# Padded small products, a first loop over three groups, a shorter rsqrt chain and new ranks in a hybrid decoder layer

## The chip, the cores and the metric

The kernel runs on one core of one Trainium2 chip. Its engines are TensorE (PE, matrix products; PEld is the loading of its weights), VectorE (DVE), ScalarE (ACT), GpSimd (POOL) and SyncE (SP, which issues most transfers). Each works through its own instructions in a fixed order and waits on counters that other engines and transfers raise. The metric is device time in microseconds of one execution, as the median over runs.

## The reference

One inference step of one layer, for a prompt of 512 tokens and for eight running sequences of one new token each (called sample), all in fp32. The columns of one input projection belong to two mixers: gated linear attention (GLA: qa, ka, va, the low-rank forget gate za and the output gate ga) and dilated attention over past keys (qb, kb, vb, gb).

```python
h = jnp.einsum('btd,de->bte', x, w_in)
qa, ka, va, za, ga, qb, kb, vb, gb = jnp.split(h, split_points, axis=-1)
log_a = jax.nn.log_sigmoid((jnp.einsum('btr,rk->btk', za, w_alpha2) + b_alpha)) / GATE_TEMP
o_a, s_new = gla_chunked(qa, ka, va, log_a, s0, chunk)        # S_t = diag(a_t) S_{t-1} + k_t^T v_t, o_t = q_t S_t
o_a = o_a * lax.rsqrt(jnp.mean(jnp.square(o_a), axis=-1, keepdims=True) + RMS_EPS) * gla_norm_g
o_b = prompt_dilated(qb, kb, vb, rel_bias)                    # sample: dilated_attention over the cache and the new row
mix = jnp.concatenate([o_a * jax.nn.silu(ga), o_b * jax.nn.silu(gb)], axis=-1)
x_new = layer_norm(DEEPNORM_ALPHA * x + jnp.einsum('bte,ed->btd', mix, w_out), ln_g, ln_b)
```

Dilated attention has 8 heads of 64; each evaluates three patterns (window, dilation) (128,1), (512,4), (2048,16) with a relative position bias from 32 buckets, and the three outputs are merged by their softmax denominators. Outputs are the new x of prompt and sample, both GLA states, and the new key and value rows.

## The kernel before

**Precision.** An fp32 product of the large projections is made of three matmuls on fp32r operands: each operand is split into a high part (a cast) and a low part (the difference), and hi x hi, lo x hi and hi x lo are added up in PSUM (`three`, line 618). The cast runs on ACT (`hi_...`, `xx<-x_raw`), the subtraction on DVE (`lo_...`, `xx<-x_raw,xx`). Small products, called here small, run directly on fp32 operands.

**Stages.** `dense` (line 691) is PE's main stream: eight matmuls on a zeroed tile for warming up (`warm_ps`), then the first loop, then za, qa, qb, kb, vb, gb, va, ga and the output projection (`ps_yf`, `ps_y`), behind which stand residual and layer norm (`norm`, line 1593). x is held transposed: 1024 rows in eight tiles of 128, with 520 columns, 512 of the prompt and 8 of sample; it is worked in two halves of 264 and 256 columns.

**The first loop** has both groups of 128 columns of ka: for each of the eight tiles of the inner dimension, two halves times two groups times three matmuls, 96 in all, on four PSUM banks. Its loads come in the order of `FIRST` (line 542), issued by SP; the first tiles of x and of the weights come in small pieces. The splits follow in the same order (`first_splits`, line 573). ACT also issues four small loads of `wz` (`clear`, line 532); its table of functions is loaded once (line 1615).

**Sample's small products.** Beside the stream stand small fp32 products: `ps_qk` (in `sample_past`), `ps_sl` and `ps_pn` (logits and new-row weights in `sample_softmax`), `ps_ov` (in `sample_gla`, whose result goes through `o_r` on DVE and a norm to a transpose, `ps_ort`), and `ps_ms` and `ps_vs` (mean and variance in `residual_sample`). Their operands have 32 or 64 rows or columns.

**Order.** All instructions but a few are issued by one line, 366, of a planner (`Plan`, line 198): the code is written as some forty tasks (Python generators) with a rank each, `add(task(), rank)`, lower first. The planner keeps a model of the engines' times and issues, at build time, the instruction that can start first; ties go by rank. `dense` has rank 100, so it fills PE wherever no other task's product is ready. So ranks alone decide where in an engine's order small work stands. `SLOTS` is the number of buffers of each size (for example `sv`, the 512 KB tiles of sample's past keys and values; `w`, split weights; `r`, raw weights; `g`, larger results), `BANKS` the PSUM banks by use. Every transfer raises one of eight counters, taken in turn (`DMAHW0` to `DMAHW7`); a transfer that is the next to use a counter waits on the queue of its issuing engine until the one before on this counter has landed.

**Sample's attention** runs past keys and values through POOL: `past` times the broadcast query (`qbc`) gives logits that DVE reduces (`lt`), then `vv` times the broadcast probabilities (`pb`) gives values that DVE reduces (`o_pv`).

**rsqrt** (line 395) is Exp(-0.5 Ln(x)) with a Newton step; in `norm` it gets `between`, the task that centres y on DVE while ACT works.

Of the kernel before, what the change touches and what calls it, by code (L numbers as in the profile page):

```python
# [59 lines left out]
N_WARM = 8  # L60

SLOTS = dict(
    g=23,
    w=6, r=3,
    sv=5,
    pt=4,
    t2=3, st=3,
    pr=6,
    t1=5, ob=4,
# [7 lines left out]
SWITCH = 105  # L77
PIECE = 256
# [116 lines left out]
class Plan:  # L195
# [3 lines left out]
    def __init__(self, nc):  # L199
        self.engines = {n: Engine(n, e) for n, e in (("PE", nc.tensor), ("DVE", nc.vector), ("ACT", nc.scalar),  # L200
                                                     ("POOL", nc.gpsimd), ("SP", nc.sync))}
        self.dma = 0.0
        self.tasks, self.marks = [], defaultdict(int)
        self.slots, self.slot_of, self.uses, self.shares = {}, {}, defaultdict(dict), {}
        self.seq = self.issued = 0
# [48 lines left out]
    def ready(self, op):  # L254
        t = 0.0
        for write, aps in ((False, op.reads), (True, op.writes)):
            for x in aps:
                _, p0, p1, f0, f1 = self.region(x, write)
                for ((w, q0, q1, g0, g1), e), end in self.uses[x.tensor.name].items():
# [3 lines left out]
                    if (w if same else w or write) and p0 < q1 and q0 < p1 and f0 < g1 and g0 < f1:  # L263
# [65 lines left out]
    def begin(self, op, ready):  # L329
# [7 lines left out]
        start = max(eng.free, ready)  # L337
# [6 lines left out]
    def issue(self, op, start):  # L344
# [12 lines left out]
        if unit == "SP":  # L357
# [4 lines left out]
            end += self.dma  # L362
        for write, aps in ((False, op.reads), (True, op.writes)):
# [7 lines left out]
def trunk(ctx: ExitStack, tc: tile.TileContext, xT, xp, xs, state, ck, cv, w_in, wab, gnorm,  # L371
# [23 lines left out]
    def rsqrt(o, x, scale, eps, between=None):  # L395

        t = yield Need("m", "newton", [P, size(x)])
        t = t[:x.ap[0][1]]
        yield V.tensor_scalar(x, x, scale, eps, op0=ALU.mult, op1=ALU.add)
        yield S.activation(o, x, AF.Ln)  # L400
        yield S.activation(o, o, AF.Exp, scale=-0.5)
        if between:

            add(between, 5)
            yield S.activation(t, o, AF.Square)
            yield S.mul(t, t, x)
            yield S.activation(t, t, AF.Copy, scale=-0.5, bias=1.5)
            yield S.mul(o, o, t)
        else:
            yield V.tensor_tensor(t, o, o, op=ALU.mult)  # L410
# [23 lines left out]
    rb = cst("rb", [66, NB, HB], F32R)  # L434
# [8 lines left out]
    lt = cst("lt", [P, 2, 64])  # L443
# [68 lines left out]
    order = [g for k, g in groups.items() if k not in ("ka0", "ka1")] + wo  # L512
# [17 lines left out]
    one16 = cst("one16", [P, 1])  # L530

    def clear():
# [5 lines left out]
        for j in range(4):  # L538
# [3 lines left out]
    FIRST = (("x", 0, TS[0]), ("w", 0, 1), ("x", 0, TS[1]), ("w", 1, 2), ("x", 1), ("w", 2, 4), ("x", 2), ("x", 3),  # L542
             ("w", 4, 6), ("x", 4), ("x", 5), ("w", 6, 8), ("x", 6), ("x", 7))
    ka_raw = []

    def first_loads():
        za = w_in[:, OFF["za"]:OFF["za"] + 16].rearrange("(k p) n -> p k n", p=P)
        for n, a, *b in FIRST:
# [5 lines left out]
            else:  # L554
                if a % 4 == 0:
                    ka_raw.append((yield Need("r", f"raw_ka{a}", [P, 4, GW])))
                rows = w_in[a * P:b[0] * P, OFF["ka"]:OFF["ka"] + GW]
                yield D.dma_start(ka_raw[a // 4][:, a % 4:a % 4 + b[0] - a, :], rows.rearrange("(k p) n -> p k n", p=P))
# [4 lines left out]
        add(weight_loads(), 3)  # L563
# [9 lines left out]
    def first_splits():  # L573
        for j, (n, a, *b) in enumerate(FIRST):
# [10 lines left out]
            else:  # L585
                if a % 4 == 0:
                    hl = []
                    for x in ("hi", "lo"):
                        hl.append((yield Need("w", f"{x}_ka{a}", [P, 4, GW], F32R)))
                    ka_hl.append(hl)  # L590
                    for i in range(2):
                        g = groups[f"ka{i}"]
                        for l, y in zip((g.hi, g.lo), hl):
                            l += [y[:, k, i * P:i * P + P] for k in range(4)]
                r = slice(a % 4, a % 4 + b[0] - a)
                yield from split(ka_raw[a // 4][:, r, :], *(y[:, r, :] for y in ka_hl[a // 4]))
                for _ in range(a, b[0]):
                    mark("kas")
                if b[0] % 4 == 0:
                    free(ka_raw[a // 4])  # L600
        add(weight_splits(), 19.3)

    def fills():
        yield V.memset(rb.bitcast(F32)[64:66], 1.0)
# [86 lines left out]
    def dense():  # L691
# [6 lines left out]
        for i in range(2):  # L698
            for u in range(2):
                pk[i, u] = yield bank("ds"[i], f"ps_ka{i}{u}")  # L700
        for k in range(KT):
            for u in range(2):
                yield At("kas", k + 1)
                yield At("xs", k + 1 + (u if k == 0 else 1))
                for i in range(2):
                    yield from three(pk[i, u][:, :TW[u]], k, halves(k, u, groups[f"ka{i}"]))
# [9 lines left out]
        add(gate_decay(pz), 10)  # L716
        yield from make("ka", Need("g", "ka", [P, 2, NP]), 3)
        yield from make("qa", Need("g", "qa", [P, 2, NP]), 2)
        for i in range(2):
            for u in range(2):  # L720
                add(into("ka", ka_s, i, 1.0)(pk[i, u], u), 2)
        for i in range(2):
            yield from feature(groups[f"qa{i}"], into("qa", qa_s, i, 0.125))
# [18 lines left out]
        for t in range(TT):  # L742
            add(residual(t), 8)
        add(residual_sample(), 8)
# [8 lines left out]
    def gate_decay(pz):  # L753
# [21 lines left out]
        for j in (0, 1, 4, 2, 3):  # L775
            z, o, to = parts_[j]
            yield S.activation(o, z, AF.Abs)
# [36 lines left out]
    def gla_levels():  # L814
# [6 lines left out]
        for li, h in enumerate(LEVELS):  # L821
# [21 lines left out]
            if li % 2:  # L843
                add(gla_level(made), 22)
# [171 lines left out]
    def parts(n, own, m, scale):  # L1016

        def evac(ps, u):
# [5 lines left out]
            yield V.scalar_tensor_tensor(l, ps[:, :256], scale, h.bitcast(F32), op0=ALU.mult, op1=ALU.subtract)  # L1024
            if u == 0:
                yield S.mul(own[:, m, :], ps[:, 256:TW[0]], scale)
            mark(f"{n}b{m}{u}")
            mark(f"{n}b")
            if n == "k":
                add(keys_out(ps, m, u), 2)  # L1030
# [25 lines left out]
    def sample_v(x, n, out):  # L1056
        yield At(n, 4)
        rows = yield Need("t1", n + "_rows", [32, P])
        yield from sample_rows(x, rows)
        yield D.dma_start(out, rows)  # L1060
# [148 lines left out]
    def sample_queries():  # L1209
# [3 lines left out]
        for bi in range(NB):  # L1213
# [4 lines left out]
            add(sample_logit(bi, past, qbc), 50)  # L1218
# [10 lines left out]
    def sample_softmax():  # L1229
        yield At("kb", 8)  # L1230
        yield At("lt", 5)
        sel = yield Need("t1", "sel", [64, C_AV - C_E2])
        yield D.dma_start(sel, c_f[:64, C_E2:C_AV])
        e2, pnm, m32 = sel[:, :P], sel[:, C_PN - C_E2:C_PN - C_E2 + 32], sel[:32, C_LN - C_E2:]
# [522 lines left out]
```

## Time and profile before

| | |
|---|---|
| time, median of 3 runs | 283.75 us (283.42 to 284.21) |
| time of the profiled execution | 282.88 us |
| its span | 281.0 us |
| mean granted PE clock | 0.992 |
| busy PE / PEld / DVE / ACT / POOL | 270.9 / 253.0 / 206.4 / 157.6 / 53.1 us |
| packets' bytes | 52.27 MB, mean 186 GB/s |

The span is the time from the first to the last instruction of the profiled execution; busy times are the sum of the instructions' durations on one engine, and overlap with each other. A row of a timeline gives the start in us from the span's start, the busy time, the engine, the line, the operation with out<-in, for PE the part of the array it uses (rows*columns), the shape of the input, how many such instructions stand in a row, and, in brackets, how long the engine was idle before and what released it. A busy time of a matmul includes its run through the array, so the start of the next one tells what it cost PE. An fp32 product counts as two matmuls.

### The profile page before, as it was taken

The page shows a single profiled execution, that of the slowest core. Times are in us where ns is not written, and L with a number is a line of the kernel's source. Part 1 is how long each engine was busy: PE and PEld are TensorE (multiplying, and loading weights), DVE is VectorE, ACT ScalarE, POOL GpSimd, SP SyncE. Part 2 cuts the span into 40 slices and gives each one's busy share as a digit, 9 for nine tenths or more (in the row PEclk, how much of TensorE's full clock was granted, in tenths as well). Part 3 has the DMA queues.
Part 4 walks back from the last instruction along what each step waited for, and adds up shares of the span by engine and source line. Part 5 has one row for each costly group of instructions (what it writes and reads, how often), then busy time and mean ns, then how long its engine had stood idle before and what let it go on. Part 6 is the DMA issues. An engine that isn't in the chain of part 4 may idle for free.

```text
span 281.0 us, 7058 instructions
## 1 busy us (share of the span) xinstructions
PE 270.9 (96%) x2760; PEld 253.0 (90%) x2760; DVE 206.4 (73%) x496; ACT 157.6 (56%) x453; POOL 53.1 (19%) x72
## 2 busy tenths in 40 slices
PE   8899999999999999999999999999999999999990
PEld 5799999999999998988879999999899999997880
DVE  4747798998969975728949966617989889239575
ACT  5747853544475856738949735425589986113011
POOL 4000000000296065400006244444400000000000
PEclk9999999999999999999999999999999999999996
DMA  6996622382894897723977398997674993976203
GB/s 190 298 241 179 200 77 77 78 225 79 236 330 148 250 306 216 223 81 88 303 210 198 111 264 207 249 224 175 221 199 125 250 264 107 240 108 200 113 27 124
DMA packets 59944, 52.27 MB, mean 186 GB/s; under 512 B 12506, under 2 KB 50692, under 8 KB 59910
## 3 DMA queue, kind: packets, MB, share of 16 engines
q1 hardware_dynamic: 59802, 51.73, 66.2%
q8 instruction: 22, 0.36, 0.6%
q14 instruction: 12, 0.10, 0.1%
q10 hardware_dynamic: 108, 0.07, 0.1%
HBM read 46.24 MB, written 6.03 MB: 186 GB/s over the span
## 4 chain that ended last, share of the span: by engine, by line
PE 90%; DVE 5%; DMA 3%; ACT 1%; issue 0%; SPq 0%; DVEq 0%
PE ps_gb L366 8%; PE ps_qb L366 8%; PE ps_yf L366 8%; PE ps_y L366 8%; PE ps_ga L366 7%; PE ps_kb L366 7%; PE ps_vb_f L366 4%; PE ps_qa L366 4%; PE ps_va_f L366 4%; PE ps_va L366 4%; PE ps_vb L366 4%; PE ps_pt L366 3%; PE ps_pv L366 3%; PE ps_s L366 3%; PE ps_ka L366 3%; DMA x_raw<-in_xT_dram 3%
## 5 line engine op out<-in xcount | busy, mean ns | idle before, releaser
L366 POOL TENSOR_TENSOR past<-past,qbc 128x256 f32<-128x256 f32 x32 | 24.9, 814 | 87.5 <-DMA past<-in_ck_dram 86.3
L366 POOL TENSOR_TENSOR vv<-vv,pb 128x256 f32<-128x256 f32 x32 | 25.0, 812 | 58.5 <-DVE mlb L366 32.2
L366 ACT ACTIVATE pr<-pr,ms 128x128 f32<-128x128 f32 (+3 forms) x47 | 24.4, 538 | 9.0 <-DVE ms L366 8.8
L366 DVE CUSTOM_DVE_ANT_0 pr<-ps_s,strip 128x128 f32<-128x128 f32 (+3 forms) x32 | 14.2, 481 | 6.7 <-PE ps_s L366 6.5
L366 PE MATMUL ps_ka<-xx,hi_ka 128*128 128x264 f32 (+1 forms) x64 | 13.6, 309 | 1.1 <-ACT xx L366 0.8
L366 ACT ACTIVATE sg<-sg 128x264 f32<-128x264 f32 (+1 forms) x32 | 13.6, 425 | 0.3
L366 PE MATMUL ps_pt<-cf,pr 128*128 128x128 f32 x80 | 13.4, 277 | 0.0
L366 PEld LDWEIGHTS ps_ka<-xx,hi_ka 128*128 128x128 f32 x64 | 11.0, 206 | 2.1 <-ACT xx L366 1.0
L366 ACT COPY pt<-ps_pt 128x128 f32<-128x128 f32 (+3 forms) x26 | 10.7, 422 | 1.1 <-PE ps_pt L366 1.0
L366 PEld LDWEIGHTS ps_pt<-cf,pr 128*128 128x128 f32 x80 | 9.2, 140 | 1.7 <-issue 1.2
L366 ACT ACTIVATE rstd<-mv 128x1 f32<-128x1 f32 x4 | 0.7, 203 | 16.6 <-DVE mv L366 16.6
L366 DVE TENSOR_REDUCE o_pv<-vv 128x4 f32<-128x1024 f32 x8 | 9.7, 1212 | 0.0
L366 DVE TENSOR_REDUCE lt<-past 128x16 f32<-128x1024 f32 x8 | 9.6, 1202 | 0.0
L366 PE MATMUL ps_pv<-pt,v 128*64 128x256 f32 (+1 forms) x96 | 9.5, 348 | 0.0
L366 PE MATMUL ps_ka<-xx,lo_ka 128*128 128x264 f32 (+1 forms) x32 | 9.4, 295 | 0.0
L366 ACT COPY feat_y<-ps_yf 128x256 f32<-128x256 f32 x8 | 2.9, 368 | 11.1 <-PE ps_yf L366 11.1
L366 PEld LDWEIGHTS ps_pv<-pt,v 128*64 128x64 f32 x96 | 6.3, 137 | 2.9
L366 DVE TENSOR_TENSOR xx<-x_raw,xx 128x520 fp32r<-128x520 f32 (+2 forms) x9 | 5.8, 640 | 3.6 <-ACT xx L366 3.5
L366 PE MATMUL ps_s<-kp,qh 64*128 64x128 f32 (+3 forms) x64 | 8.3, 344 | 0.0
L366 ACT ACTIVATE d<-d 128x512 f32<-128x512 f32 x11 | 6.6, 640 | 2.9 <-DVE d L366 2.9
L366 DVE TENSOR_SCALAR pr<-pr,ms 128x512 f32<-128x512 f32 (+2 forms) x17 | 8.1, 486 | 0.2
L366 DVE COPY_PREDICATED near<-cm,ps_l 128x256 f32<-128x256 uint8 x12 | 6.2, 544 | 1.9 <-PE ps_l L366 1.8
(530 smaller groups left out, 1031.3 us busy)
## 6 DMA issues: line engine op xcount, KB each, us to landing
past<-in_ck_dram SPq DMA_DIRECT2D x8, 512.0 KB
vv<-in_cv_dram SPq DMA_DIRECT2D x8, 512.0 KB
pb<-psd_s SPq DMA_DIRECT2D x16, 256.0 KB
s<-in_state_dram SPq DMA_DIRECT2D x4, 512.0 KB
qbc<-qsd SPq DMA_DIRECT2D x8, 256.0 KB
strip<-tabr SPq DMA_DIRECT2D x8, 256.0 KB
y<-in_xp_dram SPq DMA_DIRECT2D x4, 512.0 KB
x_raw<-in_xT_dram SPq DMA_DIRECT2D x7, 260.0 KB
```

Source lines behind the costliest of these rows:

```text
L366: getattr(eng.eng, op.fn)(*op.args, **op.kw)
```

## The change

1. Padding: sample's small products get 66 rows (`ROWS`) or more (qk 80) in place of 32 or 64, with zeros in the added ones: `rb_w`, `lt_w`, `l32`, `sums_s`, `pn_r`, `vat_rows`, `to_rows`, `avg`, `sel`, `tmp_s`. Memsets write the zeros.
2. The first loop runs over three groups, ka0, ka1 and qa1 (144 matmuls, six banks). Its weight tiles have 384 columns. The first one is loaded by ACT's queue, ahead of the table load, and its high part is made on DVE; x's second tile comes in two halves too; raw and split weights come in pairs of tiles.
3. In `rsqrt` with `between`, Ln takes scale and bias itself, DVE makes -0.5 x alongside, and ACT has one multiplication less.
4. Ranks of nearly all tasks, and four numbers of buffers, are new; the planner also models eight transfers in flight and the use of one PSUM bank by two engines.

```diff
+ROWS = 66
 SLOTS = dict(
-    g=23,
+    g=24,
     w=6, r=3,
-    sv=5,
+    sv=4,
-    pr=6,
-    t1=5, ob=4,
+    pr=4,
+    t1=5, ob=2,
...
     def rsqrt(o, x, scale, eps, between=None):
-        yield V.tensor_scalar(x, x, scale, eps, op0=ALU.mult, op1=ALU.add)
-        yield S.activation(o, x, AF.Ln)
-        yield S.activation(o, o, AF.Exp, scale=-0.5)
         if between:
+            yield S.activation(o, x, AF.Ln, scale=scale, bias=ln_eps)
+            yield V.tensor_scalar(half, x, -0.5 * scale, -0.5 * eps, op0=ALU.mult, op1=ALU.add)
+            yield S.activation(o, o, AF.Exp, scale=-0.5)
             add(between, 5)
             yield S.activation(t, o, AF.Square)
-            yield S.mul(t, t, x)
-            yield S.activation(t, t, AF.Copy, scale=-0.5, bias=1.5)
+            yield S.activation(t, t, AF.Copy, scale=half, bias=1.5)
             yield S.mul(o, o, t)
...
-    FIRST = (("x", 0, TS[0]), ("w", 0, 1), ("x", 0, TS[1]), ("w", 1, 2), ("x", 1), ("w", 2, 4), ("x", 2), ("x", 3),
-             ("w", 4, 6), ("x", 4), ("x", 5), ("w", 6, 8), ("x", 6), ("x", 7))
+    W3 = 3 * P
+    FIRST = (("x", 0, TS[0]), ("w", 0, 1), ("x", 0, TS[1]), ("x", 1, TS[0]), ("w", 1, 2), ("x", 1, TS[1]),
+             ("w", 2, 3), ("x", 2), ("w", 3, 4), ("x", 3), ("w", 4, 6), ("x", 4), ("x", 5), ("w", 6, 8), ("x", 6), ("x", 7))
...
+                yield (S if a == 0 else D).dma_start(ka_raw[a // 2][:, a % 2:a % 2 + b[0] - a, :], rows.rearrange("(k p) n -> p k n", p=P))
+                if a == 0:
+                    nc.scalar.preload_act_table_set("natural_log_exp_and_others")
...
+                if a == 0:
+                    yield V.tensor_copy(hi, raw)
+                    yield V.tensor_tensor(lo, raw, hi.bitcast(F32), op=ALU.subtract)
...
-                for i in range(2):
-                    yield from three(pk[i, u][:, :TW[u]], k, halves(k, u, groups[f"ka{i}"]))
+                for n in first:
+                    yield from three(pk[n, u][:, :TW[u]], k, halves(k, u, groups[n]))
...
-        yield T.matmul(ps[:64, 256:257], l32, one[:32], start=False, stop=False, skip_group_check=True)
+        yield T.matmul(ps[:ROWS, 256:257], l32, one[:ROWS], start=False, stop=False, skip_group_check=True)
...
-        yield T.matmul(ps[:32, 0:1], qkh.rearrange("p m u b -> p (m u b)"), one, start=True, stop=True)
+        yield T.matmul(ps[:80, 0:1], tmp[:, 2:].rearrange("p m u b -> p (m u b)"), one, start=True, stop=True)
...
-        yield T.matmul(ps[:64, 0:1], avg, sums[:, 0:1], start=True, stop=True)
+        yield T.matmul(ps[:ROWS, 0:1], avg, sums_s[:, 0:1], start=True, stop=True)
...
-    add(sample_values(), 46)
+    add(sample_values(), 47)
...
-    add(sample_gla(), 48.3)
+    add(sample_gla(), 55.3)
```

How the order changes, at three places. First, ACT's order from the start of the program, before (`wz` are the four small loads, xx is the high part of x, hi_ka of the weights; DMAHW0 is here the counter of the first load of x):

```order
L1615 ACT_TABLE_LOAD
L366 DMA wz<-in_wab_dram 18x256 [waits DVE_49]
L366 DMA wz<-in_wab_dram 18x256 x2
L366 DMA wz<-in_wab_dram 18x256 [waits DMAHW0_49]
L366 CAST xx_108<-x_raw_104 128x264
L366 CAST hi_ka_136<-raw_ka_107 128x256 [waits DMAHW1_49]
L366 CAST xx_108<-x_raw_104 128x256 [waits DMAHW2_49]
```

The same place of the change (DMAHW1 is here the counter of the first load of x, DMAHW3 of the third, which is the first half of x's second tile):

```order
L371 DMA raw_ka_109<-in_w_in_dram 128x384
L572 ACT_TABLE_LOAD
L371 DMA wz<-in_wab_dram 18x256 [waits DVE_49]
L371 DMA wz<-in_wab_dram 18x256
L371 DMA wz<-in_wab_dram 18x256 [waits DMAHW1_49]
L371 DMA wz<-in_wab_dram 18x256 [waits DMAHW3_49]
L371 CAST xx_110<-x_raw_106 128x264
L371 CAST xx_110<-x_raw_106 128x256 [waits DMAHW2_49]
L371 CAST xx_110<-x_raw_106 128x264
L371 CAST hi_ka_146<-raw_ka_109 128x384 [waits DMAHW4_49]
```

The load of the first weight tile stands ahead of the table load, and one more of the wz loads has to wait for a load of x before ACT can go on to its casts.

Second, PE's order around sample's logits, before:

```order
L366 MATMUL ps_gb_0_2068<-xx_213,hi_gb__1821 128x264
L366 MATMUL ps_pt_2080<-cf,pr_2008 128x128 x3
L366 MATMUL ps_sl<-cf,l_1759 64x1
L366 MATMUL ps_sl<-cf,lt 64x128 x2
L366 MATMUL ps_gb_0_2068<-xx_212,lo_gb__1822 128x264
```

and in the change:

```order
L371 MATMUL ps_vb_3_1945<-hi_vb__1805,xx_251 128x256
L371 MATMUL ps_sl<-cf,l_1751 66x1
L371 MATMUL ps_sl<-cf,lt 66x128 x2
L371 MATMUL ps_vb_3_1945<-lo_vb__1806,xx_251 128x256
L371 MATMUL ps_vb_3_1945<-hi_vb__1805,xx_252 128x256
```

The products have 66 rows instead of 64 and stand earlier, in vb instead of gb.

Third, DVE's order behind `ps_ov`, the second half of the steps that lead to `ps_ort`, before:

```order
L366 TENSOR_SCALAR ss_s<-rs_s 128x1 [waits DVE_49]
L366 TENSOR_REDUCE o_pv<-vv_2697 128x4 [waits DMAHW5_49,Pool_49]
L366 TENSOR_TENSOR lo_ga__2951<-raw_ga__2660,hi_ga__2950 128x1024 [waits DMAHW1_49,PE_49,Activation_49]
L366 TENSOR_TENSOR lo_ga__2979<-raw_ga__2792,hi_ga__2978 128x1024 [waits DMAHW1_49,PE_49,Activation_49]
L366 SCALAR_TENSOR_TENSOR st_2956<-st_2956,el,ps_kv_2959 128x128 [waits PE_49,Activation_49]
```

and all of these steps in the change:

```order
L371 MEMSET vat_rows 66x128
L371 TENSOR_REDUCE o_pv<-vv_2713 128x4 [waits DMAHW6_49,Pool_49]
L371 TENSOR_TENSOR o_r<-ps_ov,o_e 128x128 [waits PE_49]
L371 TENSOR_SCALAR ss_s<-ss_s 128x1 [waits Activation_49]
L371 TENSOR_TENSOR newton<-rs_s 128x1 [waits Activation_49]
L371 TENSOR_TENSOR newton<-newton,ss_s 128x1 [waits DVE_49]
L371 TENSOR_SCALAR ss_s<-rs_s 128x1 [waits DVE_49]
L371 SCALAR_TENSOR_TENSOR rs_s<-newton,ss_s 128x1 [waits DVE_49]
L371 TENSOR_SCALAR o_r<-o_r,rs_s 128x128 [waits DVE_49]
```

The steps stand together in the change, with a reduction of a product of POOL directly ahead of them; before, other work stood between them.

More of the change, by code (lines that the diff above doesn't have):

```diff
@@ L77 @@
 SWITCH = 105
+RING = 8
 PIECE = 256
@@ L697, in dense @@
         pk = {}
-        for i in range(2):
-            for u in range(2):
-                pk[i, u] = yield bank("ds"[i], f"ps_ka{i}{u}")
+        first = ("ka0", "ka1", "qa1")
+        for u in range(2):
+            for n in first:
+                pk[n, u] = yield bank(("d", "s"), f"ps_{n}{u}")
         for k in range(KT):
```

179 lines of the change are left out of this document (101 added, 78 removed).

## The prediction

> **What bounds the kernel now.** I read the page first, for its chain of work that ended last, then the timeline of TensorE (PE) for the places where it waits, then the timelines of the engines that feed those places.
>
> ```profile
> span 281.0 us, 7058 instructions
> PE 90%; DVE 5%; DMA 3%; ACT 1%; issue 0%; SPq 0%; DVEq 0%
> ```
>
> PE carries nine tenths of the chain. So a change counts only where it alters (a) the moment from which PE is continuously fed, (b) the length of PE's own stream, or (c) the few microseconds behind the last matmul. The profiled execution took 282.88 us (span 281.0, 1.88 us around it), 0.87 below the median of 283.75 of the runs shown; I work against the profiled one and carry the difference over to the median. About 0.3% (0.85 us) is what a measurement of this kernel can tell from no change.
>
> PE's timeline at the start and at the end of the first loop:
>
> ```profile
> 1.19 3.59 PE L366 MATMUL warm_ps<-warm 128*128 128x512 bf16 x8 [1.19 <-DVE warm L1617]
> 4.22 1.00 PE L366 MATMUL ps_ka<-xx,hi_ka 128*128 128x264 f32 x2
> 5.02 0.42 PE L366 MATMUL ps_ka<-xx,lo_ka 128*128 128x264 f32 x1
> ...
> 6.94 0.28 PE L366 MATMUL ps_ka<-xx,lo_ka 128*128 128x256 f32 x1
> ...
> 9.72 0.39 PE L366 MATMUL ps_ka<-xx,hi_ka 128*128 128x264 f32 x1 [0.76 <-ACT xx L366]
> 10.46 0.39 PE L366 MATMUL ps_ka<-xx,hi_ka 128*128 128x264 f32 x1 [0.35 <-DVE xx L366]
> ...
> 19.14 2.05 PE L366 MATMUL ps_za<-x_raw,zw 128*32 128x128 f32 x64
> ```
>
> A row is start, busy time, engine, line, out<-in, tile, operand; the bracket is the idle time and its releaser. Between 5.02 and 6.94 stand nine matmuls, 0.213 us each. The last 71 of the loop's 96 run from 10.46 to 19.14, 0.122 each. Just ahead of them PE is short of split operands twice (the two brackets, 1.1 us). In each later step of the inner dimension it has the data.
>
> **First loop, the good half.** One third group (qa1, 48 matmuls) moves from behind za into the loop, so each step has 18 matmuls (18 x 0.122 = 2.2 us) where it had 12 (1.5 us), for weights of 384 columns instead of 256; x, the larger load, is the same. PE therefore waits for operands less. Before, the same 144 matmuls would end at 19.14 + 48 x 0.122 = 25.0. Started at 4.22 like before and never short, the changed loop would end at 4.22 + 144 x 0.122 + 1.1 (twelve matmuls at 0.213 until 6.94) = 22.9; with half of the 1.1 us of waits left 23.5, a gain of 1.5.
>
> **First loop, the bad half.** What ACT does first decides when PE starts.
>
> ```profile
> 1.44 1.75 ACTq L366 DMA_DIRECT2D wz<-in_wab_dram  x4
> 3.22 0.41 ACT L366 CAST xx<-x_raw 128x264 fp32r<-128x264 f32 x1 [1.21 <-DMA x_raw<-in_xT_dram]
> ...
> 4.15 0.41 ACT L366 CAST xx<-x_raw 128x256 fp32r<-128x256 f32 x1
> ...
> 5.24 0.40 ACT L366 CAST hi_ka<-raw_ka 128x256 fp32r<-128x256 f32 x1 [0.69 <-DMA raw_ka<-in_w_in_dram]
> 5.97 0.62 ACT L366 CAST xx<-x_raw 128x520 fp32r<-128x520 f32 x1 [0.32 <-DMA x_raw<-in_xT_dram]
> ```
>
> ```profile
> 3.67 0.43 DVE L366 TENSOR_TENSOR xx<-x_raw,xx 128x264 fp32r<-128x264 f32 x1 [1.83 <-ACT xx L366]
> ```
>
> In before the fourth wz issue, in front of the first cast, waits for the first x load (128x264, 135 KB), which the cast needs anyway; it costs nothing. In the order of the change two wz issues wait: the third for the first x load, the fourth for the third x load. Behind it on ACT stand all casts of the first loop, and behind those DVE and PE. The loads up to that one hold 598 KB (135 + 197 of the first weight tile + 131 + 135). In before the third load (397 KB in all) was there by 4.15, the fourth (528 KB) released a cast at 5.24, the fifth (794 KB) one at 5.97. The bounds are 4.15 and 5.97; I take 5.2, since by bytes it lies behind the fourth load but the first weight load now starts on a second queue.
>
> From there: cast 0.41, then on DVE the low part of x (it starts 0.45 behind the cast's start, as 3.22 to 3.67), and then, since DVE also makes hi_ka of the first tile, a 384-column copy of some 0.45 and a subtraction of some 0.55 (estimates, by the 0.43 of 264 columns). PE's first matmul starts 1.45 after the release, 6.65 instead of 4.22, the third 1.95 after it. Two matmuls done, 142 x 0.122 = 17.3 from 7.15: the loop ends at 24.5, against 25.0: a gain of 0.5. With the release at 5.97 it ends at 25.2 (a loss of 0.2); at 4.15, with some slow matmuls until 6.94, at 23.8 (a gain of 1.2). The later loads have had that time to land.
>
> This assumes that the slow spacing ends near 6.94 as before, though PE now idles from 1.19 + 3.59 = 4.78 to 6.65. Two rows bear on it: the idle time ahead of 9.72 and 10.46 did not bring 0.213 back; but that was after the fast spacing had begun. [...]
>
> On the queues: SP issues 168 loads and stores as before. The 0.52 MB of qa1 now stand ahead of zw and the constants, which land later by
>
> ```profile
> HBM read 46.24 MB, written 6.03 MB: 186 GB/s over the span
> ```
>
> some 2.8 us at this mean; za starts 5.4 later (24.5 for 19.14), so that is covered. The last weight pair's load waits until DVE has split the first pair (three buffers), near 8.7; its use is near 20.
>
> **Padded small products.** PE's timeline around five of the six places:
>
> ```profile
> 47.98 0.28 PE L366 MATMUL ps_qb<-xx,hi_qb__454 128*128 128x256 f32 x1
> 48.19 0.22 PE L366 MATMUL ps_qk<-cf,tmp_s 128*32 128x1 f32 x2
> 48.34 0.39 PE L366 MATMUL ps_qb<-xx,hi_qb__454 128*128 128x256 f32 x1
> ...
> 130.22 0.28 PE L366 MATMUL ps_sl<-cts,rb 66*64 66x258 f32 x1
> 130.34 0.29 PE L366 MATMUL ps_gb<-xx,lo_gb__1822 128*128 128x264 f32 x1
> ...
> 131.08 0.49 PE L366 MATMUL ps_pt<-cf,pr 128*128 128x128 f32 x3
> 131.50 0.27 PE L366 MATMUL ps_sl<-cf,l 32*64 32x1 f32 x2
> 131.70 0.65 PE L366 MATMUL ps_sl<-cf,lt 128*64 128x128 f32 x4
> 132.28 0.39 PE L366 MATMUL ps_gb<-xx,lo_gb__1822 128*128 128x264 f32 x1
> ...
> 139.80 0.41 PE L366 MATMUL ps_pn<-pn_r,sel 64*128 64x32 f32 x2
> 140.14 0.39 PE L366 MATMUL ps_gb<-xx,hi_gb__2071 128*128 128x264 f32 x1
> ...
> 189.96 0.48 PE L366 MATMUL ps_ov<-vat_rows,to_rows 32*128 32x128 f32 x2
> 190.37 0.50 PE L366 MATMUL ps_va<-hi_va__2627,xx 128*128 128x256 f32 x2
> ...
> 254.07 0.27 PE L366 MATMUL ps_ms<-sums_s,avg 64*64 64x1 f32 x2
> 254.28 0.50 PE L366 MATMUL ps_y<-hi_wo__3239,mla 128*128 128x512 f32 x1
> ```
>
> Entry into qk: 48.19 - 47.98 - 0.12 = 0.09. From its start to the next: qk 0.15, the sl group 0.78, pn 0.34, ov 0.41, ms 0.21, and vs, the same product as ms, 0.21. With 0.09 of entry each: 0.24 + 0.87 + 0.43 + 0.50 + 0.30 + 0.30 = 2.64 us in which PE does 16 short passes. All are on tiles other than 128*128 on one side or both, and the next full matmul comes late. The product with 66 rows at 130.22 costs its neighbour nothing: 0.12 to the next. With the padding all six have more than 64 rows and columns. What remains is the passes. Six of 128 columns cost some 0.11 each (the three transposes from 131.08 take 0.33, with the entry 0.42): 0.65. Ten of 1 or 32 columns lie between 0.032 (za's 64 in 2.05) and 0.122; I take 0.09, nearer to the transposes, which are full-tile passes, than to za, which has a narrow tile. Left are 0.65 + 0.9 = 1.55, gained 1.1. The ends are 2.64 - 0.97 = 1.7 and 2.64 - 1.9 = 0.75, and 0 if the padding doesn't change the array's mode. These six stand in a stream that has no slack, so all of it is time. The added memsets (five on DVE at the start) lie in DVE's idle 1.83 us ahead of 3.67; the memsets of l32, tmp_s and vat_rows lie under PE.
>
> [...]
>
> **The end chain.** DVE's and ACT's timelines behind the last matmul:
>
> ```profile
> 274.71 1.40 DVE L366 SCALAR_TENSOR_TENSOR y<-y,mv,gamma 128x512 f32<-128x512 f32 x2
> ...
> 276.42 1.41 DVE L366 SCALAR_TENSOR_TENSOR y<-y,rstd,beta 128x512 f32<-128x512 f32 x2 [0.31 <-ACT rstd L366]
> ```
>
> ```profile
> 275.54 0.29 ACT L366 ACTIVATE newton<-newton,mv 128x1 f32<-128x1 f32 x1
> ```
>
> The change takes this ACT step out, and lets the first Ln start before DVE's scaling, so rstd comes some 0.45 earlier. But DVE is in the centring until 274.71 + 1.40 = 276.11; only its idle 0.31 can go, and `half` is a new DVE step of some 0.15 that stands in front of the centring: gain 0.27 (0 to 0.31).
>
> **Ranks and buffers.** They move nearly every small instruction but hardly change PE's work. One place has become tight: ps_ort waits for a chain from ps_ov through DVE and ACT.
>
> ```profile
> 190.47 0.29 DVE L366 TENSOR_TENSOR o_r<-ps_ov,o_e 128x128 f32<-128x128 f32 x1 [6.55 <-PE ps_ov L366]
> ```
>
> ```profile
> 177.67 3.27 POOL L366 TENSOR_TENSOR vv<-vv,pb 128x256 f32<-128x256 f32 x4 [2.73 <-DMA pb<-psd_s]
> 182.50 2.97 POOL L366 TENSOR_TENSOR vv<-vv,pb 128x256 f32<-128x256 f32 x4 [1.56 <-DMA pb<-psd_s]
> 190.53 2.83 POOL L366 TENSOR_TENSOR vv<-vv,pb 128x256 f32<-128x256 f32 x4 [5.07 <-DMA pb<-psd_s]
> ```
>
> PE now has some 22 matmuls and the state products between them, about 3.9 us; nine short steps of DVE and ACT at some 0.15 to 0.7 take 3.7 to 4.4. I charge 0.2 (0 to 0.5). The other moved rows I charge nothing: their cover is PE's queue of matmuls on each side.
>
> **Sum.** -0.5 (loop), -1.1 (padding), -0.27 (end), +0.2 (order) = -1.7: 281.2 in a profiled execution like the one shown, 282.1 for the median.
>
> **Rivals.**
>
> 1. ACT's block is short or costs nothing, and the loop gains its 1.5: 281.1. For it: queues that start side by side could land x early. Against: four loads have to be there.
>
> 2. The slow spacing lasts longer. From 1.19 to 6.94 it took 5.75 us of uninterrupted work before the spacing became 0.122. If the idle stretch makes this begin again at 6.65, 5.75 us hold 27 matmuls instead of 47: 2.4 us lost, less some 0.2 that the wait for lo_ka hides. If the warm-up's 3.59 us still count, 2.16 us are left, which hold 10 instead of 18: 0.9, less 0.2. Between 0.7 and 2.2 I take 1.5: the loop ends at 26.0, the sum is -0.2, the time 283.6. The idle time ahead of 9.72 and 10.46 speaks against a sensitive clock, the slow start itself speaks for it. [...]
>
> 3. Slower: DVE's o_r, and already the new memset of vat_rows that ps_ov needs, now stand behind reductions that wait for POOL's vv product. If that product comes late, ps_ort waits, and with it PE. The products came at distances from 4.8 to 8.0 us in before (182.50 to 190.53), so one may be 3.2 late: with the 0.4 by which the chain is already too long PE stands 3.6 where I charged 0.2, and the time is 282.1 + 3.4 = 285.5. It decides from a delay of about 2.3 us. For it: sv has four buffers instead of five. Against: the values' work now begins some 6 us earlier in PE's order.
>
> 4. The padding does not take the mode's cost away: +1.1, 283.2.
>
> **Chances.** Forecast 0.52, rival 1 0.10, rival 2 0.22, rival 3 0.10, rival 4 0.06. Faster by over 0.3% (below 282.9): nine tenths of the forecast's, whose own range is 281.3 to 283.0, all of rival 1, a fifth of rival 2, a third of rival 4, in all 0.62. Slower (above 284.6): a fifth of rival 2, eight tenths of rival 3 and a little of unseen waits, 0.17. Within: 0.21. The range leaves out the far ends of rivals 1 and 3: 280.6 to 284.4.
>
> **What would show it.** PE's first ps_ka matmul near 6.6 behind an idle stretch, with ACT's last wz issue ending near 5.2; za at 24.5; the spacing 0.122 from there on; the padded products without a late neighbour; DVE's idle time ahead of the last scaling gone; little idle at ps_ort. Wrong if za starts above 25.5, if a padded product still delays its neighbour, or if PE's waits list a place of over 1 us after the loop.

## The result, and the profile after

The changed kernel took 284.12 us in the median of 20 runs (281.15 to 286.49), the kernel before 283.57 (283.07 to 284.84): a ratio of 0.9998, with an interval of 0.9977 to 1.0019. Nothing was gained, and the runs spread over 5.3 us where those of before spread over 1.8. The ratio leaves out four runs that lie more than 1.5% above the fastest one, among them the execution profiled first (285.62 us, span 283.8). The rows here are of a second profiled execution (283.40 us, span 281.6) unless said otherwise; the ten runs that belong to it have a median of 283.86 and a ratio of 1.0031 (1.0013 to 1.0050). That execution stands 0.52 above the execution of before that the prediction works against.

The page, and the view of PE's waits:

```profile
span 281.6 us, 7076 instructions
...
PE 95%; DMA 2%; DVE 1%; issue 1%; ACT 0%; DVEq 0%
```

```profile
PE ps_ka L371 <- DVE hi_ka L371: 1.8, 1, 1.8
PE warm_ps L371 <- DVE warm L1647: 1.2, 1, 1.2
PE ps_l L371 <- issue: 0.7, 1, 0.7
PE ps_og L371 <- issue: 0.6, 1, 0.6
```

A row of the second view gives the engine, what it was about to write, what released it, and the time waited in all, how often, and the longest (us). PE bounds the kernel still more than before. Three of the waits are new: one ahead of the first loop, and two for which the profile names no releaser ("issue"). The two waits inside the first loop of before, 1.1 us together, are gone.

ACT's timeline at the start, and PE's from the warm-up to the end of the first loop:

```profile
1.44 3.86 ACTq L371 DMA_DIRECT2D wz<-in_wab_dram  x4
5.33 1.03 ACT L371 CAST xx<-x_raw 128x264 fp32r<-128x264 f32 x3 [2.88 <-DMA x_raw<-in_xT_dram]
```

```profile
1.19 3.60 PE L371 MATMUL warm_ps<-warm 128*128 128x512 bf16 x8 [1.19 <-DVE warm L1647]
6.63 0.78 PE L371 MATMUL ps_ka<-xx,hi_ka 128*128 128x264 f32 x2 [1.85 <-DVE hi_ka L371]
7.20 0.52 PE L371 MATMUL ps_ka<-xx,lo_ka 128*128 128x264 f32 x1
...
10.42 0.41 PE L371 MATMUL ps_ka<-xx,hi_ka 128*128 128x264 f32 x2
...
24.52 0.40 PE L371 MATMUL ps_tab<-ct,rb 66*8 66x512 f32 x1
...
25.91 0.86 PE L371 MATMUL ps_za<-x_raw,zw 128*32 128x128 f32 x22
```

The wz issues hold ACT until 5.30, the first ps_ka starts at 6.63, the slow spacing lasts until 10.0 (from 7.20 to 10.42 stand sixteen matmuls, 0.20 each), and za starts at 25.91. In before, the first loop and the third group's 48 matmuls would be through at 25.0 together. A small product that stood behind za in before, `ps_tab`, now stands ahead of it and takes 0.24 (24.52 to 24.76). So za comes 0.9 later, and on the same work the loop lost 0.7.

PE around sample's logits, and DVE at the end:

```profile
127.44 0.23 PE L371 MATMUL ps_sl<-cf,l 66*66 66x1 f32 x2
127.53 0.63 PE L371 MATMUL ps_sl<-cf,lt 128*66 128x128 f32 x4
127.91 0.36 PE L371 MATMUL ps_vb<-lo_vb__1806,xx 128*128 128x256 f32 x1
```

```profile
275.63 1.40 DVE L371 SCALAR_TENSOR_TENSOR y<-y,mv,gamma 128x512 f32<-128x512 f32 x2
277.01 1.41 DVE L371 SCALAR_TENSOR_TENSOR y<-y,rstd,beta 128x512 f32<-128x512 f32 x2
```

The padded group takes 0.47 from its start to the next product (0.78 before), and enters without a delay. DVE's idle 0.31 ahead of the last scaling is gone. From the start of PE's last matmul to the end of the span it is 7.60 us, 7.85 before.

The two standstills, in PE's timeline:

```profile
56.76 0.95 PE L371 MATMUL ps_og<-s,qx 128*32 128x128 f32 x25
58.35 0.42 PE L371 MATMUL ps_og<-s,qx 128*32 128x128 f32 x7 [0.65 <-issue]
...
76.56 1.09 PE L371 MATMUL ps_l<-qs,ka 64*64 64x32 f32 x58
78.36 0.31 PE L371 MATMUL ps_l<-qs,ka 64*64 64x32 f32 x6 [0.71 <-issue]
```

Both fall into the middle of a run of identical small products, without a wait in the program at that place. From one start to the next, 0.92 and 0.93 us pass where 0.03 and 0.015 are usual.

The balance against before, from differences of starts in the two traces:

| | before | after | |
|---|---|---|---|
| end of the 144 first matmuls (after: za 25.91 - 0.24 for `ps_tab`) | 25.0 (za 19.14 + 48 x 0.122) | 25.67 | +0.7 |
| from there to PE's last matmul, `ps_tab` included | 248.1 (253.97 - 48 x 0.122) | 248.36 | +0.25 |
| behind it | 7.85 | 7.60 | -0.25 |
| span | 280.96 | 281.62 | +0.66 |

The middle row hides two things of similar size and opposite sign: the padding, and the standstills.

### The profile page after: what moved, and what is told of

Same layout as the page of the kernel before. It is cut to its first block, busy times and chain, and to the rows that moved or that the text cites. A ratio compares the mean times of both kernels' runs of the same rounds, so it can differ in the third digit from the quotient of the medians.

```text
span 283.8 us, 7076 instructions
## 1 busy us (share of the span) xinstructions
PE 271.1 (96%) x2760; PEld 254.7 (90%) x2760; DVE 205.6 (72%) x506; ACT 155.2 (55%) x449; POOL 57.8 (20%) x72
## 4 chain that ended last, share of the span: by engine, by line
PE 94%; DMA 2%; DVE 1%; issue 1%; ACT 1%; DVEq 0%
PE ps_kb L371 9%; PE ps_ga L371 8%; PE ps_gb L371 8%; PE ps_qb L371 8%; PE ps_yf L371 8%; PE ps_y L371 8%; PE ps_ka L371 5%; PE ps_qa L371 4%; PE ps_vb_f L371 4%; PE ps_va_f L371 4%; PE ps_vb L371 4%; PE ps_va L371 4%; PE ps_pt L371 3%; PE ps_pv L371 3%; PE ps_s L371 3%; PE ps_l L371 2%
## 5 line engine op out<-in xcount | busy, mean ns | idle before, releaser
L371 POOL TENSOR_TENSOR past<-past,qbc 128x256 f32<-128x256 f32 x32 | 27.0, 877 | 90.9 <-DMA past<-in_ck_dram 87.6
L371 POOL TENSOR_TENSOR vv<-vv,pb 128x256 f32<-128x256 f32 x32 | 27.6, 892 | 53.7 <-DVE ms L371 26.0
L371 ACT COPY pt<-ps_pt 128x256 f32<-128x256 f32 (+3 forms) x25 | 10.4, 418 | 10.1 <-PE ps_pt L371 10.0
L371 PE MATMUL ps_pt<-cf,pr 128*128 128x128 f32 x80 | 14.1, 280 | 0.0
L371 DVE SCALAR_TENSOR_TENSOR y<-y,ps_yt 128x256 f32<-128x256 f32 x8 | 3.0, 418 | 11.3 <-PE ps_yt L371 11.3
L371 DVE TENSOR_SCALAR pr<-pr,ms 128x512 f32<-128x512 f32 (+3 forms) x17 | 8.9, 523 | 0.2
L371 PE MATMUL ps_kb<-xx,hi_kb__781 128*128 128x264 f32 (+1 forms) x32 | 8.5, 336 | 0.0
L371 ACT ACTIVATE rstd<-mv,ln_eps 128x1 f32<-128x1 f32 x4 | 1.2, 291 | 13.4 <-DVE mv L371 13.4
```

Source lines behind the costliest of these rows:

```text
L371: getattr(eng.eng, op.fn)(*op.args, **op.kw)
```

## The experiments

All are ratios to the kernel before on the same chip, with a 95% interval. "first ka" is the start of the first ps_ka matmul, "za" the end of the first loop (in kernels with the old loop 48 matmuls fewer), "stream" the time from za to PE's last matmul. In the change, warm, lvl and shift `ps_tab` (0.24) counts to the loop, in all others to the stream.

| | median us | ratio | first ka | za | stream |
|---|---|---|---|---|---|
| before | 283.57 | | 4.22 | 19.14 | 253.97 |
| the change, first profile | 284.12 | 0.9998 (0.9977 to 1.0019) | 7.11 | 26.65 | 249.60 |
| after2, the change once more | 283.86 | 1.0031 (1.0013 to 1.0050) | 6.63 | 25.91 | 248.12 |
| pad | 283.59 | 1.0019 (0.9996 to 1.0042) | 4.04 | 18.79 | 254.96 |
| padf | 281.53 | 0.9946 (0.9927 to 0.9964) | 4.22 | 18.62 | 252.95 |
| act | 280.79 | 0.9895 (0.9879 to 0.9911) | 4.87 | 23.10 | 250.09 |
| warm | 282.73 | 0.9973 (0.9950 to 0.9996) | 6.83 | 24.81 | 247.47 |
| lvl | 282.43 | 0.9949 (0.9930 to 0.9969) | 6.31 | 24.30 | 247.14 |
| actlvl | 279.32 | 0.9870 (0.9844 to 0.9896) | 5.01 | 22.77 | 247.12 |
| actrank | 284.87 | 1.0052 (1.0032 to 1.0073) | 5.08 | 23.54 | 252.64 |
| shift | 282.52 | 0.9956 (0.9933 to 0.9980) | 6.86 | 27.26 | 246.74 |

The starts are of one profiled execution each, the medians of 4 to 20 runs.

### The kernel once more (after2)

No edit.

> The changed kernel once more, for another profile of the same program. [...] Median 283.5 to 284.5, spread over 4 us. Rival: the profile shown was an outlier and the first matmul is at 6 or earlier.

The first matmul came at 6.63 (7.11 in the first profile). Both standstills came again, in the same products after the same number of them (25 of ps_og, 58 of ps_l), with other sizes: 0.62 and 1.54 from start to start in the first profile, 0.92 and 0.93 here. So the late start and the standstills belong to the program, their sizes to the run.

### ACT's queue (act)

```diff
-        for j in range(4):
-            yield S.dma_start(wz[j * 32:j * 32 + 18], wab[80:98])
...
         mark("zw")
+        for j in range(4):
+            yield D.dma_start(wz[j * 32:j * 32 + 18], wab[80:98])
```

> The changed kernel with the four small wz loads issued by SP behind zw instead of by ACT ahead of its casts. Theory: ACT's first cast then starts near 3.2 instead of 5.8 us, the first ps_ka matmul near 4.5 instead of 7.1, TensorE has no idle window and the first loop ends near 23.5 instead of 26.6; the time falls by 2 to 3 us against the changed kernel, to 281.0 to 282.2, and its runs lie closer together. Rival: the loads themselves are late and the first matmul stays at 6 or later; then no gain, 283.5 to 284.5.

ACT's and PE's timelines of this kernel:

```profile
3.58 0.88 ACT L371 CAST xx<-x_raw 128x264 fp32r<-128x264 f32 x2 [1.12 <-DMA x_raw<-in_xT_dram]
```

```profile
4.87 0.78 PE L371 MATMUL ps_ka<-xx,hi_ka 128*128 128x264 f32 x2
...
23.10 1.12 PE L371 MATMUL ps_za<-x_raw,zw 128*32 128x128 f32 x32
```

The first cast starts at 3.58 and the loop ends at 23.10, 2.6 earlier than the same matmuls of the change (`ps_tab` left out) and 1.9 earlier than those of before. Its ratio is 1.0% below that of the change and 1.4% below after2's, 2.9 to 3.9 us, the loop's 2.6 and something more. Its five runs lie within 2.8 us; that says little beside the 5.3 of the change's twenty and the 2.0 of after2's ten. The profiled execution, the slowest of the five (282.57), has a new wait of 1.8 us behind a softmax, as the planner has put later work in another order:

```profile
PE ps_gb L371 <- DVE ms L371: 1.8, 1, 1.8
```

So the loop over three groups does gain, and the issues in front of ACT's casts take more than all of it away. The edit moves all four of them, but the records of after2 tell them apart: the third went out at 3.58, when the first load of x was there, and ended at 3.86; the fourth, which waits for the third load, ended at 5.30. By these times the fourth costs most of what is lost.

### The idle stretch and the slow spacing (warm)

```diff
-N_WARM = 8
+N_WARM = 13
```

> The changed kernel with 13 instead of 8 warm-up matmuls, so that TensorE idles little before its first ps_ka matmul. Theory: the slow spacing at the start of the first loop comes from the idle stretch ahead of it; with it filled, the loop runs at 0.12 us from its first or second step and ends 1.0 to 1.5 us earlier: 282.6 to 283.2. Rival: the spacing is decided by the loads or by the loop itself; then 284.

PE's timeline:

```profile
1.19 5.23 PE L371 MATMUL warm_ps<-warm 128*128 128x512 bf16 x13 [1.19 <-DVE warm L1647]
6.83 0.48 PE L371 MATMUL ps_ka<-xx,hi_ka 128*128 128x264 f32 x2 [0.41 <-DVE hi_ka L371]
7.33 0.39 PE L371 MATMUL ps_ka<-xx,lo_ka 128*128 128x264 f32 x1
7.56 0.41 PE L371 MATMUL ps_ka<-xx,hi_ka 128*128 128x264 f32 x2
7.80 0.28 PE L371 MATMUL ps_ka<-xx,lo_ka 128*128 128x264 f32 x1
```

The first ps_ka is 0.2 later than in after2, the spacing is 0.12 from 7.56 on, and the loop ends at 24.81, 1.1 earlier. That is the price of the idle stretch's slow clock in these two executions, apart from the late start itself. By the ratios, warm is 0.25 to 0.6% (0.7 to 1.6 us) below the change; the smaller figure lies within the intervals.

The view by windows of the first profile of the change shows the clock. Its stretches are us, PE busy (x), PEld, DVE, ACT, POOL, PEclk, DMA share and GB/s:

```profile
0.90:4.31 3.41, 3.12 (x8) 1.01 (x8) 0.99 (x10) 1.28 (x1) 2.81 (x4) 1.00 0.71 210
4.32:7.72 3.40, 0.88 (x5) 0.41 (x4) 1.43 (x4) 1.91 (x6) 0.00 (x0) 1.00 0.87 247
7.73:11.13 3.40, 3.40 (x16) 3.40 (x17) 3.34 (x8) 1.92 (x4) 0.00 (x0) 0.50 0.98 299
...
75.99:79.40 3.41, 2.09 (x124) 1.94 (x125) 2.64 (x7) 1.42 (x7) 3.33 (x4) 1.00 1.00 371
79.41:82.81 3.40, 3.40 (x20) 3.33 (x20) 2.92 (x6) 1.09 (x4) 3.11 (x5) 0.50 0.83 232
```

PEclk is 1.00 in the first row only because the profile has no record of the clock ahead of 4.31; the warm-up's matmuls are 0.427 apart there, and 0.217 in warm behind its first record, so by the spacing the clock was low until then. PEclk is 0.50 in the rows 7.73:11.13 and 79.41:82.81. Ahead of the first stand 3.40 us with PE busy for 0.88, ahead of the second 3.41 us that hold the standstill of ps_l, with PE busy for 2.09. The first of these half-clock stretches of 3.40 us fits 16 matmuls of the loop instead of the 28 of 0.122: 1.5 us. In the second execution the clock had not yet risen when the idle stretch came: PE was busy for 1.59 of the 3.41 us ahead of 6.60, and the first record of a full clock is at 10.01, where before has it at 6.90. In the profile of lvl the same idle stretch is 1.5 long:

```profile
2.05:5.46 3.41, 2.73 (x7) 0.70 (x5) 0.03 (x1) 0.85 (x3) 1.66 (x2) 1.00 0.92 290
5.47:8.87 3.40, 2.54 (x19) 2.36 (x20) 3.20 (x8) 2.44 (x7) 0.00 (x0) 1.00 0.87 253
```

There the first record of a full clock is at 5.46, PEclk is 1.00 until 8.87, and the loop ended at 24.30. That first record lies at another time in each profile (4.31, 10.01 and 5.46 in these three). So an idle stretch of 1.5 to 2.5 us cost nothing in the clock of lvl and some 1.5 us in each of the two executions of the change. What decides between the two was not shown. This is not where the change's spread of 5.3 us comes from: of its twenty runs the slowest (286.49) has the highest mean granted clock, 0.996, and the fastest (281.15) has 0.992. Where the spread comes from stays open.

### One rank (lvl)

```diff
-                add(gla_level(made), 41.7)
+                add(gla_level(made), 22)
```

> The changed kernel with one rank put back: gla_level at 22 instead of 41.7, so the blocks of ps_l stand earlier. Theory: the 1.3 us in which TensorE stands still inside the last ps_l block near 78 us, and the slow clock behind it, belong to that block's place beside the loads of past, strip and vb; without it 1 to 2.5 us less than the changed kernel, 281.7 to 283. Rival: the standstill goes to another block and the time stays at 284.

```profile
PE ps_ka L371 <- DVE hi_ka L371: 1.5, 1, 1.5
...
PE ps_og L371 <- issue: 0.6, 1, 0.6
```

The standstill in ps_l is gone, the one in ps_og has stayed, and the ratio is 0.5 to 0.8% (1.4 to 2.3 us) below those of the change. The stream is 1.0 shorter; the rest of this execution's gain is the loop (24.30 instead of 25.91), where the clock stayed up (PEclk 1.00 from 5.47 to 8.87). It is the fastest of the six runs (280.81; the median is 282.43), so its gain is not that of all six.

### Where the standstills come from (shift)

PE's instruction records (matmuls, weight loads and waits) were counted from the program's start in every profile. They stood at these numbers when a standstill without a releaser began:

```
after, after2, act      ps_og  1217    ps_l  1985
lvl, actlvl             ps_og  1217
warm                                   ps_l  1985
actrank                 ps_l   1217
padf                    ps_qb  1473
```

Each is a multiple of 256 plus 193. The waits with a releaser that are as long stand elsewhere (for example 69, 129 and 176 beyond a multiple). The page lists 22 packets, 0.36 MB together, on a queue of kind "instruction". Each has 16,384 bytes. In the first profile 196 of PE's 5,582 records had started when the first packet had landed and 5,560 when the last had: 255 for each packet between. So the author's estimate is that a packet brings a block of 256 of PE's instructions. Each standstill ended 1.27 to 1.62 us after such a packet had landed. warm has the order of the change and ten records more ahead of it, five matmuls with their weight loads. Its standstill in ps_l keeps the number and comes five products earlier, after 53 instead of 58:

```profile
74.91 0.98 PE L371 MATMUL ps_l<-qs,ka 64*64 64x32 f32 x53
76.25 0.42 PE L371 MATMUL ps_l<-qs,ka 64*64 64x32 f32 x11 [0.36 <-issue]
```

The same holds in ps_og, where a break of 0.28 from start to start, too short for the view of waits, comes after 20 products instead of 25. So the place goes by the number of the instruction, not by the product. In the window of the standstill in ps_l of the first profile the other transfers moved 371 GB/s (row 75.99:79.40 above).

The next edit puts 128 records in ahead of all these places:

```diff
+        for _ in range(64):
+            nc.tensor.matmul(warm_ps[:32, :16], warm[:32, :32], warm[:32, :16], start=True, stop=True)
```

behind the warm-up; the order on every engine is that of the change.

> The changed kernel, every engine's order kept, with 64 tiny matmuls (32 rows, 16 columns, 128 instructions with their weight loads) behind the warm-up, in the stretch in which TensorE idles anyway. Theory: the standstills without a releaser in ps_og and ps_l stand at TensorE's instruction number 193 beyond a multiple of 256, the end of a fetched block of 16,384 bytes, because such a block then consists of nothing but fast small products. Moved by 128 instructions, each block holds some 80 slow ones, and both standstills (0.6 to 0.9 and 0.9 to 1.5 us) go or fall below 0.3; the time falls by 1 to 2.5 us to 281.5 to 282.8, some of it by the slow clock. Rival: the standstills belong to the operands or the banks of these products; then they stay at the same product, and the time stays near 284.

PE's timeline at the four places:

```profile
4.71 1.87 PE L720 MATMUL warm_ps<-warm 32*32 32x16 bf16 x64
6.86 0.56 PE L371 MATMUL ps_ka<-xx,hi_ka 128*128 128x264 f32 x1 [0.27 <-DVE hi_ka L371]
...
58.11 1.08 PE L371 MATMUL ps_og<-s,qx 128*32 128x128 f32 x32
...
76.94 1.11 PE L371 MATMUL ps_l<-qs,ka 64*64 64x32 f32 x64
```

All 32 products of ps_og and all 64 of ps_l now run through, with the same operands, banks, neighbours and loads. What was changed is the number at which each product stands among PE's records, 128 higher, and the time at which the stream starts. The stream is 246.74 instead of 248.12, although a wait for a softmax (ps_s, 1.0 from start to start) has come in. With warm this shows the number of the instruction as the place, and speaks against the rival of the operands and the banks. In the first profile the 256 records ahead of the standstill in ps_og are 104 products of ps_l and 25 of ps_og and start within 2.3 us; those ahead of the one in ps_l are 122 of ps_l and 6 of kb, within 2.7. What PE waits for behind them was not shown: no run changes the packets alone, and that it is PE's next instructions is the author's estimate from the landings. Such records alone do not bring a standstill: in shift the 256 records up to 1729, again 193 beyond a multiple of 256, hold 116 products of ps_l and 12 of kb, and PE goes on at once, the last packet having landed 3.2 us before. What makes a packet come when it does, and what part the other transfers have in that, stays open. The ratio is 0.4 to 0.8% (1.2 to 2.1 us) below those of the change, although the loop ended at 27.26 in this execution.

### The padding, with a new order and with the old one (pad, padf)

pad is the kernel before with part 1 of the change alone; the planner, whose model charges for a change between tiles, puts everything in a new order. padf has the same products and tells the planner the old sizes, for example:

```diff
-        yield T.matmul(ps[:64, 0:1], avg, sums[:, 0:1], start=True, stop=True)
+        yield T.matmul(ps[:ROWS, 0:1], avg, sums_s[:, 0:1], start=True, stop=True, small=(64, 64))
```

> The kernel before with the padding alone (ranks, buffers, first loop and rsqrt as before). Theory: the six padded products give back 1.1 to 1.4 us of TensorE time whatever else happens, so 282.2 to 282.5 us against 283.57, and each padded product's neighbour follows within 0.12 us. Rival: what the padding gives back is lost again in the first wait behind it; then 283.3 to 283.8 us.

> The kernel before with the padding alone, and with the planner told the old sizes, so that every engine's order is that of before (the added memsets aside). Theory: the run with the padding and a new order lost in new waits (ps_oat 1.5, ps_yf 1.0, the first loop 0.7 more) what the padded products gave back; with the order kept the 1.6 us show: 281.7 to 282.3. Rival: the padded products are shorter but the stream waits for something else, so 283.2 to 283.8.

The waits of PE in pad:

```profile
PE ps_oat L367 <- DVE oa L367: 1.5, 1, 1.5
...
PE ps_yf L367 <- DVE oa L367: 0.7, 1, 0.7
PE ps_yf L367 <- DVE ga L367: 0.3, 1, 0.3
```

and PE's timeline of padf at two of the products:

```profile
131.29 0.49 PE L377 MATMUL ps_pt<-cf,pr 128*128 128x128 f32 x3
131.62 0.23 PE L377 MATMUL ps_sl<-cf,l 66*66 66x1 f32 x2
131.71 0.63 PE L377 MATMUL ps_sl<-cf,lt 128*66 128x128 f32 x4
132.10 0.37 PE L377 MATMUL ps_gb<-xx,lo_gb__1830 128*128 128x264 f32 x1
...
189.36 0.39 PE L377 MATMUL ps_ov<-vat_rows,to_rows 66*128 66x128 f32 x2
189.50 0.48 PE L377 MATMUL ps_va<-hi_va__2634,xx 128*128 128x256 f32 x2
```

In padf the six take 0.10 (qk), 0.48 (sl), 0.14 (pn), 0.14 (ov), 0.09 and 0.09 (ms, vs) us, 1.04 in all, where it was 2.64: 1.6 us less. The stream is only 1.0 shorter, since a standstill without a releaser has come in (0.97 from start to start, in ps_qb, at record 1473); -1.6 and +0.85 make -0.75, and 0.3 more went at places that were not traced. The medians have 0.54%, 1.5 us (1.0 to 2.1), 0.5 of which this execution has in its first loop (18.62 for 19.14). In pad the products are as short, and the new order loses all of it in 2.5 us of waits near the output projection.

### The ranks, and both mends (actrank, actlvl)

actrank is act with every rank of before. actlvl is act and lvl together.

> The changed kernel with the wz loads on SP and with all ranks of tasks as in before (numbers of buffers as changed). If the new ranks are worth time, this is slower than with the new ranks (280.8): 282 or more; if they cost time (the standstill in ps_l, the wait at ps_gb), it is faster: 279.5 to 280.5. In both cases the first loop ends near 23.1.

```profile
PE ps_yf L371 <- ACT oa L371: 3.3, 1, 3.3
...
PE ps_l L371 <- issue: 1.0, 1, 1.0
```

The loop ends at 23.54, as it should, and the stream is 252.64, 2.6 longer than that of act and 5.5 longer than that of actlvl: PE stands for 3.3 us at the output projection, since the work on oa comes late, and a stretch of half clock follows (PEclk 0.50 from 232.48 to 235.88). By the ratios it is 1.6% (4.4 us) above act, which has the new ranks. So the new ranks together are worth several us to this structure; the one that was shown to cost is gla_level's.

> Both edits on the changed kernel: wz loads on SP behind zw, and gla_level's rank back at 22. Theory: the first removes 2.9 us at the start, the second the standstill in ps_l, and they add up: 279.5 to 280.8. Rival: they remove the same loss (the slow clock), and the time stays with that of the first alone, 280.8, or the new order brings a new wait, 281 to 282.

```profile
PE ps_og L371 <- issue: 0.5, 1, 0.5
PE ps_ka L371 <- DVE hi_ka L371: 0.2, 1, 0.2
```

With both edits it is 279.32 us, 1.3% (1.0 to 1.6%) faster than before, and the four runs lie within 1.1 us. The forecast was that the two gains add up, and by the ratios they don't in full: the second edit brings 0.25% (0.7 us) beyond act, less than the 0.5 to 0.8% that lvl has over the change, and the intervals of act and actlvl overlap. It fits that the standstill in ps_l, which the second edit removes, was only 0.5 from start to start in act's profile. Of the kernels measured this is the fastest. What PE still stands for behind the warm-up is the 0.5 without a releaser in ps_og and 0.2 ahead of the loop.

## Why the prediction was wrong

It said 282.1 (280.6 to 284.4) with a chance of 0.62 for faster; measured was 284.12, no change by the interval. The time lies inside the range, but the gain of 1.7 did not come. The case that came is its second rival, to which it gave 0.22 and 283.6, with one cost on top that it did not see. That 283.6 is so near to what was measured is luck: 1.8 us of standstills are not in it, and a larger gain from the padding and a smaller loss in the loop hide half of that.

- **ACT's issue in front of the casts: right.** Release expected at 5.2, measured 5.30 (5.77 in the first profile, within the bounds of 4.15 and 5.97); first matmul 6.65 and 6.63; third 7.15 and 7.20. act shows that without ACT's issues the loop ends at 23.10, between the 22.9 and 23.5 of the prediction's good half, and with them at 25.67.
- **"This assumes that the slow spacing ends near 6.94 as before": the step that failed first.** It ended at 10.0 (11.1 in the first profile). The loop ended at 25.67 (25.91 with `ps_tab`), not 24.5; the rival had 26.0. The rows quoted against it (idle time ahead of 9.72 and 10.46) showed 1.1 us of idle time with work on both sides, behind the rise of the clock at 6.90; the change idles 1.85 to 2.5 at a stretch, ahead of the rise (10.01 in the second execution) or just behind it (4.31 in the first). The rival's price, 1.5, is what the half-clock stretch of 3.40 us cost in the first profile.
- **Padding: the gain came, its size was forecast too small.** 1.1 forecast, 1.6 measured in padf. The term that was most off is "ten of 1 or 32 columns ... I take 0.09": the ten took 0.51 in padf instead of 0.9 (ps_ms, two passes, 0.09 in all), which is near the za row, not the transposes. The six of 128 columns took 0.53 instead of 0.65. The upper end, 1.7, was nearly right. In the change itself it is 1.5, since ps_pn there stands behind a product on another tile (ps_s, 64*128) and takes 0.24 to the next start instead of 0.14.
- **End chain: right.** -0.27 forecast, -0.25 measured, in all seven kernels with it (7.58 to 7.60 against 7.83 to 7.85).
- **"The other moved rows I charge nothing: their cover is PE's queue of matmuls on each side": the second step that failed.** The order cost 1.8 us (second execution) and 2.1 us (first) in the standstills of ps_og and ps_l, start to start, and 1.5 more, an estimate by the loop's half-clock stretch, where one followed (row 79.41:82.81). PE's queue of matmuls does not cover them; the profile names no releaser, and what PE waited for was not shown. ps_ort, to which 0.2 was charged, cost nothing: it started 0.12 after its neighbour, and rival 3 did not come. Rival 4 was wrong too.

With the measured sizes the sum for the second execution is +0.7 - 1.5 - 0.25 + 1.8 = +0.75, against 0.66 between the spans.

## What to carry to other kernels

An issue that waits for a load must not stand on an engine's queue in front of the work that the first loads are meant to feed (with act, which moves all four, the loop ended 2.6 us earlier); ask of each transfer which counter it takes, and who stands behind it. Where PE idles between a warm-up and the first product, warm up until the operands are there: with warm the loop ended 1.1 us earlier than in after2, since the slow spacing that followed the idle stretch was gone; in lvl no such spacing followed. An edit that shortens a few instructions should be measured with the order kept, since a planner's new order can cost more than the edit gives (1.6 us gained by the products, 2.5 us of waits in pad).

## What was unexpected of the hardware

In eight of the eleven profiles PE stood still, for 0.3 to 1.3 us idle, at a place for which the profile names no releaser (the view of waits has "issue"). The numbers of these places among PE's own records are 1217, 1473 and 1985, each 193 beyond a multiple of 256, and the 256 records ahead are mostly products of 0.016 to 0.03 us. Those of ps_l and ps_og came five products earlier when ten instructions were put in ahead (warm), and went when 128 were put in (shift).

In shift, 64 tiny matmuls kept PE busy from 4.71 to 6.58, and yet the slow spacing lasted until 12.8; five more large ones (warm) had the fast spacing by 7.6. In shift PE was busy for 3.41 us of the 3.41 ahead of 5.98, over a third of it with tiny products, and for 3.13 of the 3.40 behind that, and from 9.40 to 12.80 only 18 matmuls fit; in lvl it was busy for 2.73 of the 3.41 us ahead of 5.46, with large products alone, and had a full clock from there. So in this one profile more busy time in the trace did not bring an earlier rise of the clock; whether that is due to the small size of the products was not shown.
